# Second attention by pairs of heads: one float32 group per pair, exponentials ahead of the copies, ten projection steps before the first group

## The chip, the cores and the metric

The kernel runs on one core of a Trainium2 chip. The metric is the device time of one execution in microseconds (us). The core has a matrix engine (PE, with its weight loads PEld), a vector engine (DVE), an activation engine (ACT), a general engine (POOL, which also issues some DMAs) and a queue (SP) that issues most DMAs. Each works through its own instructions in order.

## What is computed

A two-layer decoder trunk on 256 positions of width 1024, all in float32. Each layer is a half-step SwiGLU feed-forward, a token mixer, and a second feed-forward, each with an RMS norm that is modulated by a conditioning vector. The mixer of the first layer is differential attention; the mixer of the second, which the change concerns, is forgetting attention with 16 heads of 64, keys `k`, values `v` and gates `F` shared and computed before:

```python
def forgetting_attention(h, w_q, w_o, k, v, F):
    q = (h @ w_q).reshape(b, s, B_HEADS, HEAD_DIM)
    ...
    def block(args):                       # 128 queries
        causal = q_pos[:, None] >= k_pos[None, :]
        decay = jnp.transpose(Fqb, (0, 2, 1))[..., None] - F_k[:, :, None, :]
        logits = jnp.einsum('bqhd,bkhd->bhqk', qb, k) * scale + decay
        logits = jnp.where(causal, logits, -jnp.inf)
        p = jax.nn.softmax(logits, axis=-1)
        return jnp.einsum('bhqk,bkhd->bqhd', p, v)
    ...
    return o.reshape(b, s, B_WIDTH) @ w_o
```

## The kernel before

Activations are held transposed: 128 features on the partitions, 256 positions along the free axis. A large product is made of three single-pass matmuls (`mm3`): weights and activations are each split into a high part (`wh`, `HH`, `obh`) and a rest (`wl`, `HL`, `obl`) in a rounded format, fp32r, and high x high, low x high and high x low are summed. The attention's own products (scores, transposes, values) run in full float32, each matmul as two instructions in the trace, transposes as one.

Weights stream in as pieces of 128x1024. For each, ACT casts `wh` from the raw piece and DVE subtracts to get `wl`. These background instructions are placed by a planner at emission (`bg`, `fill_act`, `fill_dve`): `InOrder` wraps PE, ACT, DVE and SP, keeps a running estimate of each engine's time, and puts a piece's cast or subtraction where it expects room. POOL isn't wrapped. What is emitted to an engine runs in that order.

The second attention (`attention_b`) stands between two feed-forwards. `late_pairs` projects q for the first eight heads (q0, q1) while the norm's factor is still being computed; meanwhile DVE and ACT make the modulated activations `HH` and `HL`, eight slices in turn (`MakeH`: `ht` and `HL` on DVE, `HH` on ACT), and at the end q1. Then 19 rounds `t` follow, one head per stage of a pipeline: the decay of head t+1 (DVE adds the key's gate `fkb`, which POOL's queue has loaded as 256 columns on all partitions, the query's gate `Fq` and the causal mask), the normalisation of head t-1 (DVE), the scores of head t (two matmuls over 64 rows, `sb`), DVE's reduction for the row maximum and ACT's exponentials, the transposes of head t-2 (`pwb`, copied by ACT to `wtb`), the values of head t-3 (`pob`, with v stationary and the weights moving). A pair's output is cast (`obh`) and subtracted (`obl`) in one piece each. `PLAN` says how many projection steps (`fills`) go before and after the scores in each round: 16 steps of six matmuls for q2 and q3 (heads 8 to 15), then 48 steps of three matmuls for the output projection (`OutProj.steps`, `pw`), which go through the first six pairs. `OutProj.finish` takes the last two pairs, with 48 matmuls. All instructions of PE, ACT, DVE and SP are recorded by a helper at L103, so the profile tells them apart by tiles.

The first attention (`attention_a`) is already written in groups: two 64-row halves' scores in turn (`s`), transposes (`pw<-tri,nl`), values with the transposed weights stationary (`po<-va,wt`), transposes of the output (`po<-tri,on`).

PSUM banks: `mmbank` has four, `sbank` (`sb`) two, `abank` and `bbank` one each.

Of the kernel before, what the change touches and what calls it, by code (L numbers as in the profile page):

```python
# [22 lines left out]
AH = 8  # L23
BH = 16
# [5 lines left out]
BIG = 3.0e38  # L30
# [9 lines left out]
CP_FIT = 0.9  # L40
DVE_FIT = 0.6
NFILL = 1
FRONT = 0
TAIL = 4
PLAN = [1, 1, 1, 1, 2, 1, 2, 3, 1, 3]
PACE = [0.62, 0.74, 0.62, 0.38, 0.76, 0, 0.74]
NRAW = 6
NLO = 5
# [59 lines left out]
def trunk(ctx, tc, a, out):  # L108
    nc = tc.nc
    InOrder.ready = {}  # L110
    pe = InOrder(tc, nc.tensor, 0.0, 1 / 2350)
    act = InOrder(tc, nc.scalar, 0.13, 1 / 1200)
    dve = InOrder(tc, nc.vector, 0.08, 1 / 960)
    sp = InOrder(tc, nc.sync, 0.0, 1 / 704)
    cp_ = ctx.enter_context(tc.tile_pool(name="cp", bufs=1))
# [15 lines left out]
    def bbank(name):  # L131
        return pp.tile([P, 512], F32, tag="tb", name=name)

    mm = pe.matmul
# [685 lines left out]
    QT = ((0, 128), (128, 256))  # L820
# [4 lines left out]
    ident, cmask, ub, skew, nlam, subg = (late[n] for n in ("ident", "cmask", "ub", "skew", "nlam", "subg"))  # L825
# [174 lines left out]
    op = attention_a()  # L1000
# [5 lines left out]
    kT = [cp_.tile([P, 512], F32, name=f"kT{j}") for j in range(4)]  # L1006
    vb = [[cp_.tile([P, 512], F32, name=f"vb{t}{nh}") for nh in range(2)] for t in range(2)]
# [17 lines left out]
    pz = sbank("pzf")[:, :S]  # L1025
# [13 lines left out]
    for i, (kk, n) in enumerate(v_proj("wkv", vb)):  # L1039
# [9 lines left out]
        if i == 3:  # L1049
# [4 lines left out]
            Fq = cp_.tile([P, 72], F32, name="Fq")[:, :2 * BH]  # L1054
# [6 lines left out]
            fdram = tc.dram_tile([BH, S], F32, name="fdram")  # L1061
# [12 lines left out]
    def attention_b():  # L1074
        ohs = [cp_.tile([P, 512], F32R, tag=f"hidh{j}", name=f"obh{j}") for j in range(4)]
        ols = [cp_.tile([P, 512], F32R, tag=f"hidl{4 + j}", name=f"obl{j}") for j in range(4)]
        o = [(ohs[c // 2][:, (c % 2) * 256:(c % 2) * 256 + 256],
              ols[c // 2][:, (c % 2) * 256:(c % 2) * 256 + 256]) for c in range(NC)]
        q = [cp_.tile([P, 512], F32, tag=f"hidl{j}", name=f"q{j}") for j in range(4)]
        gs, ds, sms = {}, {}, {}  # L1080

        def load_g(hd):
            g = cp_.tile([P, S], F32, tag=("hidh10", "hidl10", "hidl8", "hidl9")[hd % 4], name=f"fkb{hd}")
            nc.gpsimd.dma_start(g, bass.AP(fdram.tensor, fdram.offset + hd * S, [[0, P], [1, S]]))
            gs[hd] = g

        def decay(hd):
            d = cp_.tile([P, 384], F32, tag=f"hidh{4 + hd % 4}", name=f"d{hd}")
            for qt, (c0, w) in enumerate(QT):
                dve.scalar_tensor_tensor(  # L1090
                    d[:, c0:c0 + w], gs[hd][:, :w], Fq[:, qt * BH + hd:qt * BH + hd + 1], cmask[:, S - w:],
                    op0=ALU.add, op1=ALU.add)
            ds[hd] = d
            if hd + 4 < BH:
                load_g(hd + 4)

        late_pairs("wq", q[:2], ((1, 4), (1, 3)), AF.Exp)
        for hd in range(4):
            load_g(hd)
        decay(0)  # L1100
        op = OutProj(o)
        st = {}
        pob = {}
        mode[0] = "fill"

        def scores(hd):
            c, m = hd // 2, hd % 2
            rows = slice(m * HD, m * HD + HD)
            cb = (c % 2) * 256
            d = ds[hd]  # L1110
            s = sbank(f"sb{hd}")
# [3 lines left out]
            nm = kp.tile([P, 2], F32, tag="nm", name=f"nmb{hd}")  # L1115
            sm = kp.tile([P, 2], F32, tag="sm", name=f"smb{hd}")
            for qt, (c0, w) in enumerate(QT):
                dve.tensor_tensor_reduce(
                    d[:, c0:c0 + w], s[:, c0:c0 + w], d[:, c0:c0 + w], -0.125, BIG,
                    ALU.add, ALU.min, accum_out=nm[:, qt:qt + 1])  # L1120
                act.activation(d[:, c0:c0 + w], d[:, c0:c0 + w], AF.Exp,
                               bias=nm[:, qt:qt + 1], scale=-1.0, accum_out=sm[:, qt:qt + 1])
            sms[hd] = sm

        def normal(hd):
            d = ds[hd]
            rs = kp.tile([P, 2], F32, tag="rs", name=f"rsb{hd}")
            dve.reciprocal(rs, sms[hd])
            for qt, (c0, w) in enumerate(QT):
                dve.tensor_scalar(d[:, c0:c0 + w], d[:, c0:c0 + w], rs[:, qt:qt + 1], None, op0=ALU.mult)  # L1130

        def weights_t(hd):
            pw = abank(f"pwb{hd}")
            for b in range(3):
                pe.transpose(pw[:, b * P:b * P + P], ds[hd][:, b * P:b * P + P], ident)
            wt = cp_.tile([P, 384], F32, tag=f"hidh{8 + hd % 2}", name=f"wtb{hd}")
            act.copy(wt, pw[:, :384])
            st[hd] = wt

        def values(hd):  # L1140
            c, m = hd // 2, hd % 2
            rows = slice(m * HD, m * HD + HD)
            if m == 0:
                pob[c] = bbank(f"pob{c}")
            po, wt = pob[c], st[hd]
            vs = slice((hd % 8) * HD, (hd % 8) * HD + HD)
            v0, v1 = vb[0][hd // 8][:, vs], vb[1][hd // 8][:, vs]
            mm(po[rows, 128:256], v1, wt[:, 256:384], start=True, stop=False, skip_group_check=True)
            mm(po[rows, 0:256], v0, wt[:, 0:256], start=False, stop=True, skip_group_check=True)
            if m == 1:  # L1150
                oh, ol = o[c]
                act.copy(oh, po[:, :256])
                dve.tensor_tensor(ol, po[:, :256], oh.bitcast(F32), op=ALU.subtract)

        def fills():
            for j in (2, 3):
                yield from pair_proj("wq", q[j], f"pq{j}")
            for _ in range(6):
                yield from op.steps()

        fill = fills()

        def step(n):
            for _ in range(n):
                next(fill, None)

        step(FRONT)
        for t in range(BH + 3):
            n0, n1 = PLAN[2 * (t // 4):2 * (t // 4) + 2]
            step(n0)  # L1170
            if t + 1 < BH:
                decay(t + 1)
            if 0 <= t - 1 < BH:
                normal(t - 1)
            if t < BH:
                scores(t)
            step(n1)
            if 0 <= t - 2 < BH:
                weights_t(t - 2)
            if 0 <= t - 3 < BH:  # L1180
                values(t - 3)
        for i, n in fill:
            if i % 4 == 3:
                run_laters()
# [138 lines left out]
```

## Time and profile before

| | us |
|---|---|
| median of 3 runs | 1005.78 (1005.42 to 1006.49) |
| the profiled execution | 1006.43 |
| its span, first to last instruction | 1004.7 |
| first matmul behind late_pairs | 739.5 |
| last head's values end, projections alone from here | 805.6 |
| first matmul of the last feed-forward | 812.7 |

The granted clock is 0.997 over the span. Start times in the rows count from the span's first instruction. In a row of the timeline the duration of a matmul reaches from its start to its modelled end; matmuls are pipelined, so what one costs is read from the distance of starts. A row of the groups ends with busy us, mean ns of one, then the idle time before and who ended it.

### The profile page before, as it was taken

How to read it: one execution, taken by the hardware profiler on the slowest of the kernel's cores; microseconds unless marked ns; L12 is line 12 of the kernel's file. 1: busy time of each engine (PE TensorE's matmuls, PEld its weight loads, DVE VectorE, ACT ScalarE, POOL GpSimd, SP SyncE). 2: the span in 40 equal slices, each digit the busy share in tenths (PEclk: the TensorE clock that was granted, in tenths of full speed). 3: DMA queues.
4: the chain of work that ended last, by engine and by line, in shares of the span. 5: the costliest groups of instructions: out<-in, count | busy, mean ns of one | idle time of the engine just before them, and what ended most of it. 6: DMA issues, size and time to landing. Idle time of an engine off the chain costs nothing.

```text
span 1004.7 us, 20432 instructions
## 1 busy us (share of the span) xinstructions
PE 979.0 (97%) x8076; PEld 941.3 (94%) x8076; DVE 820.9 (82%) x1379; ACT 563.3 (56%) x922; POOL 37.1 (4%) x64
## 2 busy tenths in 40 slices
PE   5999999999999999999999999999999999999996
PEld 4999999988989999999988999999987799999996
DVE  6989979889889998888698988889897787555553
ACT  5465545575877645455476455454575576454552
POOL 0000100000111000000000000000011010000000
PEclk9999999999999999999999999999999999999998
DMA  8988999958765899888757999989744337665661
GB/s 347 414 333 285 334 364 345 348 199 320 264 211 196 272 403 356 288 283 308 275 191 304 363 339 327 331 296 336 245 147 122 107 125 236 198 193 153 172 183 43
DMA packets 68131, 265.08 MB, mean 264 GB/s; under 512 B 7961, under 2 KB 8113, under 8 KB 57922
## 3 DMA queue, kind: packets, MB, share of 16 engines
q1 hardware_dynamic: 65810, 258.31, 73.3%
q0 software_dynamic: 1792, 4.81, 1.8%
q8 instruction: 63, 1.03, 0.4%
q10 hardware_dynamic: 432, 0.64, 0.2%
q14 instruction: 34, 0.28, 0.1%
HBM read 262.66 MB, written 2.65 MB: 264 GB/s over the span
## 4 chain that ended last, share of the span: by engine, by line
PE 92%; DVE 3%; ACT 2%; issue 1%; DMA 1%; SPq 0%; POOL 0%; DVEq 0%; POOLq 0%; ACTq 0%
PE po L103 24%; PE pg L103 21%; PE pu L103 21%; PE pf L103 5%; PE pv L103 4%; PE pw L103 4%; PE lp L103 2%; PE pqk L103 2%; PE pk L103 1%; PE pob L103 1%; PE lg L103 1%; PE lu L103 1%; PE sb L103 1%; DVE wl L103 1%; DMA ada<-in_ada 1%
## 5 line engine op out<-in xcount | busy, mean ns | idle before, releaser
L103 DVE TENSOR_TENSOR wl<-raw,wh 128x1024 fp32r<-128x1024 f32 (+1 forms) x368 | 401.3, 1104 | 92.8 <-issue 24.7
L103 ACT CAST wh<-raw 128x1024 fp32r<-128x1024 f32 (+1 forms) x368 | 349.3, 958 | 208.7 <-PE pu L103 96.5
L103 DVE CUSTOM_DVE_ANT_0 ada<-ada,cact,vecs 128x1024 f32<-128x1024 f32 x160 | 203.3, 1278 | 0.0
L103 PE MATMUL po<-hidl,wh 128*128 128x256 f32 x704 | 194.3, 276 | 0.0
L103 PE MATMUL po<-hidh,wh 128*128 128x256 f32 x704 | 194.3, 276 | 0.0
L103 PE MATMUL po<-hidh,wl 128*128 128x256 f32 x704 | 194.3, 276 | 0.0
L103 PE MATMUL pg<-HH,wh 128*128 128x256 f32 x608 | 168.1, 276 | 0.0
L103 PE MATMUL pg<-HH,wl 128*128 128x256 f32 x608 | 168.0, 276 | 0.0
L103 PE MATMUL pg<-HL,wh 128*128 128x256 f32 x608 | 168.0, 276 | 0.0
L103 PE MATMUL pu<-HH,wl 128*128 128x256 f32 x608 | 167.9, 276 | 0.0
L103 PE MATMUL pu<-HH,wh 128*128 128x256 f32 x608 | 167.9, 276 | 0.0
L103 PE MATMUL pu<-HL,wh 128*128 128x256 f32 x608 | 167.9, 276 | 0.0
L103 PEld LDWEIGHTS po<-hidh,wh 128*128 128x128 f32 x704 | 132.2, 188 | 0.0
L103 PEld LDWEIGHTS po<-hidh,wl 128*128 128x128 f32 x704 | 132.2, 188 | 0.0
L103 PEld LDWEIGHTS po<-hidl,wh 128*128 128x128 f32 x704 | 132.2, 188 | 0.0
L103 PEld LDWEIGHTS pg<-HH,wh 128*128 128x128 f32 x608 | 114.2, 188 | 0.7 <-issue 0.6
L103 PEld LDWEIGHTS pg<-HH,wl 128*128 128x128 f32 x608 | 114.2, 188 | 0.0
L103 PEld LDWEIGHTS pu<-HL,wh 128*128 128x128 f32 x608 | 114.2, 188 | 0.0
L103 PEld LDWEIGHTS pu<-HH,wl 128*128 128x128 f32 x608 | 114.1, 188 | 0.0
L103 PEld LDWEIGHTS pg<-HL,wh 128*128 128x128 f32 x608 | 114.1, 188 | 0.0
L103 PEld LDWEIGHTS pu<-HH,wh 128*128 128x128 f32 x608 | 114.1, 188 | 0.0
L103 ACT ACTIVATE HH<-ht,modall 128x256 fp32r<-128x256 f32 x56 | 27.8, 507 | 40.4 <-DVE ht L103 38.9
(204 smaller groups left out, 1604.7 us busy)
## 6 DMA issues: line engine op xcount, KB each, us to landing
raw<-in_win SPq DMA_DIRECT2D x176, 512.0 KB, 5.9
ada<-in_ada SPq DMA_DIRECT2D x79, 1024.0 KB, 7.4
raw<-in_wout SPq DMA_DIRECT2D x64, 384.0 KB, 4.9
raw<-in_wout SPq DMA_DIRECT2D x64, 320.0 KB, 4.3
raw<-in_wqk SPq DMA_DIRECT2D x16, 512.0 KB, 5.0
raw<-in_wo SPq DMA_DIRECT2D x16, 512.0 KB, 5.2
raw<-in_wv SPq DMA_DIRECT2D x8, 512.0 KB, 7.4
raw<-in_wkk SPq DMA_DIRECT2D x8, 512.0 KB, 8.1
```

The source lines that it names most:

```text
L103: return self.tc.keep_in_program_order(f(*args, **kw))
```

## The change

The second attention is rewritten like the first one, with a pair of heads in place of a head:

- `scores` writes the causal mask of the diagonal blocks into both banks with two fp32r matmuls (identity x mask), then adds four float32 score matmuls, the two heads' row halves in turn. Two ACT copies (`identr`, `maskr`) behind `late_pairs` make the operands.
- `decay` moves to POOL, as one `tensor_scalar` per block (key's gate plus query's gate, no mask), and loads 512 columns per pair.
- The weights are no longer normalised on DVE; `divide` scales a pair's output by the reciprocal sums.
- `values` makes the transposed weights stationary and moves 64 columns of v, so the output comes with positions on the partitions, and two more transposes (`out_t`) turn it; `out_split` casts and subtracts in two halves.
- One group per pair holds scores, transposes, values and output transposes of four successive pairs without a projection step between. On ACT and DVE `exps` comes first, then `out_split`, then the copies.
- Eleven groups with 10, 8, 8, 6, 7, 7, 7, 7, 7, 6 and 5 steps before them; a step of q2 and q3 counts as two.

```diff
-FRONT = 0
-TAIL = 4
-PLAN = [1, 1, 1, 1, 2, 1, 2, 3, 1, 3]
...
+        identr = cp_.tile([P, P], F32R, tag="hidl8", name="identr")
+        maskr = cp_.tile([P, P], F32R, tag="hidl9", name="maskr")
+        def load_g(c):
+            g = cp_.tile([P, 512], F32, tag=("hidh10", "hidl10")[c % 2], name=f"fkb{c}")
+            nc.gpsimd.dma_start(g, bass.AP(fdram.tensor, fdram.offset + 2 * c * S, [[0, P], [1, 2 * S]]))
...
-        def decay(hd):
-            d = cp_.tile([P, 384], F32, tag=f"hidh{4 + hd % 4}", name=f"d{hd}")
-            for qt, (c0, w) in enumerate(QT):
-                dve.scalar_tensor_tensor(
-                    d[:, c0:c0 + w], gs[hd][:, :w], Fq[:, qt * BH + hd:qt * BH + hd + 1], cmask[:, S - w:],
-                    op0=ALU.add, op1=ALU.add)
+        def decay(c):
+            for m in range(2):
+                hd = 2 * c + m
+                d = cp_.tile([P, 384], F32, tag=f"hidh{4 + hd % 4}", name=f"d{hd}")
+                for qt, (c0, w) in enumerate(QT):
+                    nc.gpsimd.tensor_scalar(d[:, c0:c0 + w], gs[c][:, m * S:m * S + w],
+                                            Fq[:, qt * BH + hd:qt * BH + hd + 1], None, op0=ALU.add)
...
         late_pairs("wq", q[:2], ((1, 4), (1, 3)), AF.Exp)
+        act.copy(identr, ident)
+        act.copy(maskr, cmask[:, P:])
...
+        def scores(c, sb):
+            cb = (c % 2) * 256
+            m2 = maskr.rearrange("p (o k) -> p o k", o=1).to_broadcast([P, 2, P])
+            for m in range(2):
+                diag = sb[m].rearrange("p (a b) -> p a b", b=256)[:, :, :P]
+                mm(diag, identr, m2, start=True, stop=False, skip_group_check=True)
             for qt, (c0, w) in enumerate(QT):
-                mm(s[:, c0:c0 + w], q[c // 2][rows, cb + qt * P:cb + qt * P + P],
-                   kT[c // 2][rows, cb:cb + w], start=True, stop=True)
+                for m in range(2):
+                    rows = slice(m * HD, m * HD + HD)
+                    mm(sb[m][:, c0:c0 + w], q[c // 2][rows, cb + qt * P:cb + qt * P + P],
+                       kT[c // 2][rows, cb:cb + w], start=False, stop=qt == 1, skip_group_check=True)
...
-        def normal(hd):
-            dve.reciprocal(rs, sms[hd])
-            for qt, (c0, w) in enumerate(QT):
-                dve.tensor_scalar(d[:, c0:c0 + w], d[:, c0:c0 + w], rs[:, qt:qt + 1], None, op0=ALU.mult)
...
+        def values(c, po):
+            for m in range(2):
+                ...
+                mm(po[:, m * HD:m * HD + HD], wt[0], v0, start=True, stop=True)
+                mm(po[:, P + m * HD:P + m * HD + HD], wt[1], v0, start=True, stop=False)
+                mm(po[:, P + m * HD:P + m * HD + HD], wt[2], v1, start=False, stop=True)
...
+        def group(t):
+            ...
+            if cs is not None:
+                scores(cs, sb)
+            if cw is not None:
+                weights_t(cw, ta, tb)
+            if cv is not None:
+                values(cv, tb[:, 256:])
+            if co is not None:
+                pz = [sb[m][:, 384:] for m in range(2)]
+                out_t(co, pz)
+            if cs is not None:
+                exps(cs, sb)
+            if co is not None:
+                out_split(co, pz)
+            if cw is not None:
+                weights_out(cw, ta, tb)
+            if cv is not None:
+                divide(cv, tb[:, 256:])
+            if t + 1 < NP:
+                decay(t + 1)
...
+        for t, n in enumerate((10, 8, 8, 6, 7, 7, 7, 7, 7, 6, 5)):
+            for _ in range(n):
+                next(fill)
+            group(t)
```

PE before, one round in the middle of the attention (`sb` scores, `pq` a projection step, `pwb` transposes, `pob` values):

```order
L103 MATMUL sb_9600<-kT_6350,q_9247 128x128
L103 MATMUL sb_9600<-kT_6350,q_9247 128x256
L103 MATMUL pq_9580<-HH,wh 128x256
L103 MATMUL pq_9580<-HH,wl 128x256
L103 MATMUL pq_9580<-HL,wh 128x256
...
L103 MATMUL pwb_9617<-tri,d_9476 128x128 x3
L103 MATMUL pob_9577<-wtb_9575,vb_6355 64x128
L103 MATMUL pob_9577<-wtb_9575,vb_6353 64x256
```

PE after the change, group 4 (masks, scores, `wa` and `wb` transposes and values, `onb` the output's first transpose):

```order
L100 MATMUL sb_0_9771<-maskr,identr 128x2x128
L100 MATMUL sb_1_9772<-maskr,identr 128x2x128
L100 MATMUL sb_0_9771<-kT_6351,q_9248 128x128
L100 MATMUL sb_1_9772<-kT_6351,q_9248 128x128
L100 MATMUL sb_0_9771<-kT_6351,q_9248 128x256
L100 MATMUL sb_1_9772<-kT_6351,q_9248 128x256
L100 MATMUL wa_9773<-tri,d_9659 128x128 x3
L100 MATMUL wa_9773<-tri,d_9662 128x128
L100 MATMUL wb_9774<-tri,d_9662 128x128 x2
L100 MATMUL wb_9774<-vb_6353,wta_9724 128x64 x2
L100 MATMUL wb_9774<-vb_6355,wta_9724 128x64
...
L100 MATMUL sb_0_9771<-tri,onb_9730 128x128
```

The two heads' scores alternate between two banks behind two masks, and no projection stands inside (the other value matmuls are left out, and a second `onb` transpose follows).

ACT at the end of late_pairs, before (`lcol` and `q` finish q1):

```order
L103 COPY lcol<-lp_9323 128x1
L103 ACTIVATE q_9247<-lt,lcol 128x256 x2
L103 CAST wh<-raw 128x1024
L103 ACTIVATE d_9436,smb_9457<-d_9436,nmb_9456 128x128
L103 ACTIVATE d_9436,smb_9457<-d_9436,nmb_9456 128x256
```

and after:

```order
L100 COPY lcol<-lp_9325 128x1
L100 ACTIVATE q_9247<-lt,lcol 128x256 x2
L100 CAST identr<-tri 128x128
L100 CAST maskr<-tri 128x128
L100 CAST wh<-raw 128x1024
L100 ACTIVATE d_9436,smb_9488<-d_9436,nmb_9487 128x128
```

The copies of the identity and of the mask stand behind q1 and ahead of the first exponentials.

POOL at the start of the attention, before nothing but loads (`fkb`), and after:

```order
L1084 DMA fkb_9432<-fdram 128x512
L1084 DMA fkb_9434<-fdram 128x512
L1093 TENSOR_SCALAR d_9436<-fkb_9432,Fq 128x128
L1093 TENSOR_SCALAR d_9436<-fkb_9432,Fq 128x256
L1093 TENSOR_SCALAR d_9439<-fkb_9432,Fq 128x128
L1093 TENSOR_SCALAR d_9439<-fkb_9432,Fq 128x256
L1084 DMA fkb_9442<-fdram 128x512
L1093 TENSOR_SCALAR d_9499<-fkb_9434,Fq 128x128
```

The first two pairs' decays need only the loads; that of the third waits for the first pair's transposes, since it reuses their tiles.

More of the change, by code (lines that the diff above doesn't have):

```diff
@@ L1080, in attention_b @@
         gs, ds, sms = {}, {}, {}
[L1082 to L1085, printed above, removed]
-        def decay(hd):
-            d = cp_.tile([P, 384], F32, tag=f"hidh{4 + hd % 4}", name=f"d{hd}")
-            for qt, (c0, w) in enumerate(QT):
-                dve.scalar_tensor_tensor(
-                    d[:, c0:c0 + w], gs[hd][:, :w], Fq[:, qt * BH + hd:qt * BH + hd + 1], cmask[:, S - w:],
-                    op0=ALU.add, op1=ALU.add)
-            ds[hd] = d
-            if hd + 4 < BH:
-                load_g(hd + 4)
+        identr = cp_.tile([P, P], F32R, tag="hidl8", name="identr")
[3 more added lines that the diff above has]
+            nc.gpsimd.dma_start(g, bass.AP(fdram.tensor, fdram.offset + 2 * c * S, [[0, P], [1, 2 * S]]))
+            gs[c] = g
+        def decay(c):
[5 more added lines that the diff above has]
+                                            Fq[:, qt * BH + hd:qt * BH + hd + 1], None, op0=ALU.add)
+                ds[hd] = d
+            if c + 2 < BH // 2:
+                load_g(c + 2)
         late_pairs("wq", q[:2], ((1, 4), (1, 3)), AF.Exp)
-        for hd in range(4):
-            load_g(hd)
+        act.copy(identr, ident)
+        act.copy(maskr, cmask[:, P:])
+        for c in range(2):
+            load_g(c)
         decay(0)
@@ L1102, in attention_b @@
         st = {}
-        pob = {}
         mode[0] = "fill"
-        def scores(hd):
-            c, m = hd // 2, hd % 2
-            rows = slice(m * HD, m * HD + HD)
+        NP = BH // 2
+        def scores(c, sb):
             cb = (c % 2) * 256
-            d = ds[hd]
-            s = sbank(f"sb{hd}")
+            m2 = maskr.rearrange("p (o k) -> p o k", o=1).to_broadcast([P, 2, P])
+            for m in range(2):
+                diag = sb[m].rearrange("p (a b) -> p a b", b=256)[:, :, :P]
+                mm(diag, identr, m2, start=True, stop=False, skip_group_check=True)
@@ L1140, in values @@
[L1140 to L1153, printed above, removed]
+                for m in range(2):
+                    rows = slice(m * HD, m * HD + HD)
+                    mm(sb[m][:, c0:c0 + w], q[c // 2][rows, cb + qt * P:cb + qt * P + P],
+                       kT[c // 2][rows, cb:cb + w], start=False, stop=qt == 1, skip_group_check=True)
@@ new lines, in exps @@
+        def exps(c, sb):
+            nm = kp.tile([P, 4], F32, tag="nm", name=f"nmb{c}")
+            sm = kp.tile([P, 4], F32, tag="smb", name=f"smb{c}", bufs=3)
+            for m in range(2):
+                d = ds[2 * c + m]
+                for qt, (c0, w) in enumerate(QT):
+                    cc = 2 * qt + m
+                    dve.tensor_tensor_reduce(
+                        d[:, c0:c0 + w], sb[m][:, c0:c0 + w], d[:, c0:c0 + w], -0.125, BIG,
+                        ALU.add, ALU.min, accum_out=nm[:, cc:cc + 1])
+                    act.activation(d[:, c0:c0 + w], d[:, c0:c0 + w], AF.Exp,
+                                   bias=nm[:, cc:cc + 1], scale=-1.0, accum_out=sm[:, cc:cc + 1])
+            sms[c] = sm
@@ new lines, in weights_t, with weights_out @@
+        def weights_t(c, ta, tb):
+            for j in range(6):
+                d, b = ds[2 * c + j // 3], j % 3
+                pe.transpose(ta[:, j * P:j * P + P] if j < 4 else tb[:, (j - 4) * P:(j - 3) * P],
+                             d[:, b * P:b * P + P], ident)
+        def weights_out(c, ta, tb):
+            w0 = cp_.tile([P, 512], F32, tag="hidh8", name=f"wta{c}")
+            w1 = cp_.tile([P, 256], F32, tag="hidh9", name=f"wtb{c}")
+            act.copy(w0, ta)
+            dve.tensor_copy(w1, tb[:, :256])
+            st[c] = [w0[:, j * P:j * P + P] for j in range(4)] + [w1[:, j * P:j * P + P] for j in range(2)]
@@ new lines, in values @@
+        def values(c, po):
+            for m in range(2):
+                hd = 2 * c + m
+                wt = st[c][3 * m:3 * m + 3]
+                vs = slice((hd % 8) * HD, (hd % 8) * HD + HD)
+                v0, v1 = vb[0][hd // 8][:, vs], vb[1][hd // 8][:, vs]
+                mm(po[:, m * HD:m * HD + HD], wt[0], v0, start=True, stop=True)
+                mm(po[:, P + m * HD:P + m * HD + HD], wt[1], v0, start=True, stop=False)
+                mm(po[:, P + m * HD:P + m * HD + HD], wt[2], v1, start=False, stop=True)
@@ new lines, in divide, with out_t @@
+        def divide(c, po):
+            rs = kp.tile([P, 4], F32, tag="rs", name=f"rsb{c}")
+            dve.reciprocal(rs, sms[c])
+            on = kp.tile([P, 256], F32, tag="w512b", name=f"onb{c}")
+            dve.tensor_tensor(on.rearrange("p (g d) -> p g d", g=4), po.rearrange("p (g d) -> p g d", g=4),
+                              rs.rearrange("p (g o) -> p g o", o=1).to_broadcast([P, 4, HD]), op=ALU.mult)
+            st[c] = on
+        def out_t(c, pz):
+            for qt in range(2):
+                pe.transpose(pz[qt], st[c][:, qt * P:qt * P + P], ident)
@@ new lines, in out_split @@
+        def out_split(c, pz):
+            oh, ol = o[c]
+            for qt in range(2):
+                act.copy(oh[:, qt * P:qt * P + P], pz[qt])
+            for qt in range(2):
+                qs = slice(qt * P, qt * P + P)
+                dve.tensor_tensor(ol[:, qs], pz[qt], oh[:, qs].bitcast(F32), op=ALU.subtract)
+        def group(t):
+            cs, cw, cv, co = (c if 0 <= c < NP else None for c in (t, t - 1, t - 2, t - 3))
+            sb = [sbank(f"sb{t}_{m}") for m in range(2)] if cs is not None or co is not None else None
+            ta = abank(f"wa{t}") if cw is not None else None
+            tb = bbank(f"wb{t}") if cw is not None or cv is not None else None
+            if cs is not None:
[17 more added lines that the diff above has]
+                decay(t + 1)
@@ L1155, in fills @@
         def fills():
             for j in (2, 3):
-                yield from pair_proj("wq", q[j], f"pq{j}")
+                for _ in pair_proj("wq", q[j], f"pq{j}"):
+                    yield
+                    yield
             for _ in range(6):
-                yield from op.steps()
+                for _ in op.steps():
+                    yield
         fill = fills()
-        def step(n):
+        for t, n in enumerate((10, 8, 8, 6, 7, 7, 7, 7, 7, 6, 5)):
             for _ in range(n):
-                next(fill, None)
@@ L1167, in attention_b @@
[L1167 to L1184, printed above, removed]
+                next(fill)
@@ L1185, in attention_b @@
+            group(t)
+        for _ in fill:
+            pass
         return op
```

18 lines of the change are left out of this document (removed).

## The prediction

> **What bounds the kernel now.** I read first the busy time by stretch. Its row for most of the second attention (start and end in us, its length, then busy us and instructions of PE, PEld, DVE, ACT and POOL, clock, DMA share, GB/s):
>
> ```profile
> 768.00:806.00 38.00, 38.00 (x241) 28.28 (x240) 25.71 (x83) 20.16 (x56) 1.69 (x3) 1.00 0.36 109
> ```
>
> PE is busy all 38 us at full clock, DVE 68%, ACT 53%, POOL 4%, DMA 36%. Then the waits of PE between 735 and 813 us (who waited, for whom; total, times, longest):
>
> ```profile
> PE sb L103 <- DVE nmb L103: 1.0, 1, 1.0
> PE pwb L103 <- ACT wtb L103: 0.5, 1, 0.5
> ```
>
> Only 1.5 us can come back from waits; anything more must come out of PE's own work. Third, the chain of waits through one head (start, us, what):
>
> ```profile
> 757.30 0.85 PE sb L103 x4
> 758.14 0.90 PE pq L103 x6
> 759.04 0.33 PE pwb L103 x3
> 759.37 0.80 PE pob L103 x4
> 760.16 0.90 PE pq L103 x6
> 761.06 0.85 PE sb L103 x4
> ```
>
> The chain never leaves PE: scores, a projection step, transposes, values, a step. A head costs 761.06 - 757.30 = 3.76 us with 12 projection matmuls in it. Last, PE's timeline at the first matmul behind late_pairs, in the closing run of projections, and where the feed-forward takes over:
>
> ```profile
> 739.48 0.28 PE L103 MATMUL pq<-HH,wh 128*128 128x256 f32 x1
> ...
> 806.01 0.28 PE L103 MATMUL pw<-obh,wh 128*128 128x256 f32 x1
> ...
> 812.72 0.28 PE L103 MATMUL lg<-HH,wh 128*128 128x258 f32 x1
> ```
>
> From 806.01 to 812.72 are 57 projection matmuls: 0.118 us each. The stage is 812.72 - 739.48 = 73.2 us. In it are 96 matmuls for q2 and q3, 144 in the six output steps and 48 in finish, 288 x 0.118 = 33.9 us, which stay. The heads' own PE time is 73.2 - 33.9 - 1.5 = **37.8 us**, 2.36 a head. The single head agrees: 3.76 - 12 x 0.118 = 2.34.
>
> **PE after the change.** The first attention already works as the new code does: scores of two 64-row halves in turn, and values with the transposed weights stationary. One of its groups on PE's timeline:
>
> ```profile
> 251.72 0.28 PE L103 MATMUL pqk<-HL,wh 128*128 128x256 f32 x1
> 251.93 0.93 PE L103 MATMUL s<-qk 64*128 64x128 f32 x8
> 252.79 0.55 PE L103 MATMUL pw<-tri,nl 128*128 128x128 f32 x3
> 253.17 0.83 PE L103 MATMUL po<-va,wt 128*128 128x128 f32 x6
> 253.84 0.38 PE L103 MATMUL po<-tri,on 128*128 128x128 f32 x2
> ...
> 254.18 0.28 PE L103 MATMUL pqk<-HH,wl 128*128 128x256 f32 x1
> ```
>
> Eight score instructions take 252.79 - 251.93 = 0.86 us, as long as the four of one head above (0.85): the two halves run side by side. The whole group takes 254.18 - 251.72 less two projection matmuls, 2.22 us, with 3 transposes, 6 value instructions and 2 transposes of the output. The new pair adds to this: two mask matmuls, 0.24 if they cost what a 256-column projection matmul costs; three more transposes, 0.33 by the pwb row; six more value instructions. Those stream 64 columns, a width that the trace lacks; the rows on both sides are 128 columns (0.67 us for six, 253.17 to 253.84) and 16:
>
> ```profile
> 529.21 0.73 PE L103 MATMUL pF<-lft,tri 128*128 128x16 f32 x6
> 529.88 0.39 PE L103 MATMUL pFk<-tri,lft 128*16 128x128 f32 x2
> ```
>
> Six take 0.67 us there too, so 64 columns cost the same 0.112 each. Sum: 2.22 + 0.24 + 0.33 + 0.67 = 3.46 us a pair against 4.7, eight pairs 27.7, and 0.2 for group 0, whose scores go straight back to projections: 27.9. **PE's work falls by 37.8 - 27.9 = 9.9 us.** For the masks, a form that the trace lacks, the cheap end is 0.12 and the dear end the float32 price of the sb row (0.85 us for 384 columns), 0.57: up to 0.9 more a pair. I take the cheap end, since operands and width are those of a projection matmul.
>
> **The waits.** The two old ones go: the bank that freed late (sb) and the copy that the transposes waited for (pwb) were both DVE and ACT starting heads behind a queue, and group 1 now comes eight steps after group 0. What is late next is the start. PE reaches group 0 after ten steps, 30 matmuls: 739.48 + 3.54 = 743.0. Its first instruction reads maskr, which ACT copies behind q1. The rows for q1, and the nearest to a 128x128 copy on ACT (from the groups, mean ns):
>
> ```profile
> 744.01 0.91 ACT L103 ACTIVATE q<-lt,lcol 128x256 f32<-128x256 f32 x2 [0.84 <-DVE lt L103]
> L103 ACT ACTIVATE on<-po 128x128 f32<-128x128 f32 x16 | 4.1, 260 | 2.1 <-PE po L103 2.1
> ```
>
> 744.92 + 2 x 0.26 = 745.4, so PE waits **2.4 us**, with everything behind it: its queue is in order, and q's steps 5 to 7, which could run, stand behind the masks.
>
> And q1 may itself come later. The decays move from DVE to POOL, and the first two pairs' eight tensor_scalars run during late_pairs, as soon as the first loads land (DMA issues: median us to landing) and POOL has started them:
>
> ```profile
> 726.12 1.22 POOL L1084 DMA_DIRECT2D fkb<-fdram  x2 [194.21 <-PE po L103]
> fkb<-fdram POOLq DMA_DIRECT2D x4, 128.0 KB, 5.6
> L442 POOL TENSOR_TENSOR acc<-acc,sq 128x256 f32<-128x256 f32 x10 | 7.9, 790 | 1.7 <-ACT sq L103 1.1
> L1017 POOL MEMSET fgh<- 128x512 f32 x2 | 1.1, 529 | 171.5 <-PE po L103 171.5
> ```
>
> Not before 731.7. A 256-column tensor_scalar lies between the memset's 0.26 and the two-input add's 0.79; four of a pair (768 columns) between 0.8 and 2.4 us. DVE is then on the chain that makes HH, HL and q1, without a gap (period 0.92, two instructions of 0.48):
>
> ```profile
> 737.39 0.48 DVE L103 SCALAR_TENSOR_TENSOR ht<-x,modall,r 128x256 f32<-128x256 f32 x1
> 738.31 0.49 DVE L103 SCALAR_TENSOR_TENSOR ht<-x,modall,r 128x256 f32<-128x256 f32 x1
> ...
> 810.94 0.57 DVE L103 SCALAR_TENSOR_TENSOR HL<-x,modall,HH 128x256 fp32r<-128x256 f32 x1
> 813.09 0.56 DVE L103 SCALAR_TENSOR_TENSOR HL<-x,modall,HH 128x256 fp32r<-128x256 f32 x1
> ```
>
> The last two stand beside POOL's adds, and are 0.08 longer. The adds:
>
> ```profile
> 810.42 0.80 POOL L442 TENSOR_TENSOR acc<-sq,sq 128x256 f32<-128x256 f32 x1 [34.94 <-ACT sq L103]
> 812.57 0.80 POOL L442 TENSOR_TENSOR acc<-acc,sq 128x256 f32<-128x256 f32 x1
> ```
>
> HL ended at 811.51 and 813.65, 0.28 to 0.29 after the adds' ends at 811.22 and 813.37: it looks held until POOL is done, then runs. So a POOL instruction beside this chain costs up to its length. The chain's scaling starts at 735.7; I reckon that decay(0) is through by then and decay(1) partly not: between 0 and 2.4 us, I take **1.0**. [...]
>
> Third, group 3 is followed at once by output step 0, which needs the pair that group 3 has only just transposed. Before, at the last pair, PE's values and what followed on ACT and DVE:
>
> ```profile
> 804.76 0.86 PE L103 MATMUL pob<-wtb,vb 128*64 128x128 f32 x4
> 805.66 0.37 ACT L103 CAST obh<-pob 128x256 fp32r<-128x256 f32 x1 [1.68 <-PE pob L103]
> 806.07 0.42 DVE L103 TENSOR_TENSOR obl<-pob,obh 128x256 fp32r<-128x256 f32 x1 [2.38 <-ACT obh L103]
> ```
>
> obl ended 0.87 us after the values. With casts and subtractions in halves about the same: 0.8 us of wait after group 3, which no step separates, 0.5 after group 4 (one step of 0.35 us), 0.1 after group 5, none later: **1.4**. That the exponentials stand ahead of these casts on ACT costs nothing, as four of them end about when out_t does.
>
> POOL later: decay(t+1) may start when group t's transposes are done, about 1.9 us into it, and is read 1.2 us into group t+1; the period is 3.46 + 7 x 0.353 = 5.9, which leaves 5.2 us for 0.8 to 2.4. DVE loses decay and normalisation work, and the weight splits ride on it with room. The stages behind are PE's alone and only start earlier.
>
> **Sum:** -9.9 - 1.5 + 2.4 + 1.0 + 1.4 = -6.6 us. The profiled execution took 1006.43 (span 1004.7), which gives 999.8; from the median of the runs, 1005.78, it is 999.2. I give 999.5.
>
> **Rivals.** (1) *Fewer new waits.* POOL is through before the chain starts, and the casts come in half the time: 1.0 + 0.7 less, 997.8. For it: 4 us lie between landing and 735.7. Against: the held HL rows. (2) *A long idle makes PE slow.* At the program's start PE came from an idle of 3.8 us and ran at half rate:
>
> ```profile
> 17.12 0.41 PE L103 MATMUL pf<-HH,wh 128*128 128x256 f32 x1
> 17.33 0.41 PE L103 MATMUL pf<-HH,wl 128*128 128x256 f32 x1
> ...
> 22.24 0.32 PE L103 MATMUL pf<-HH,wh 128*128 128x256 f32 x1
> ```
>
> 0.21 a matmul from 17.12 to 22.24, 24 of them, each 0.095 dearer: 2.3 us. [...] Against: the two waits in this stage were too short to show it. [...] (3) *The PE saving isn't had*: the score halves don't overlap when they add onto a mask (8 x 0.86 = 6.9), or the masks cost float32's price (8 x 0.9 = 7.2): about 1006.6. Against: the first attention's rows; for it, no matmul there adds onto a bank already written. (4) *POOL sets the period*, and the kernel is slower. It decides from the point where a pair's decays and load issue (0.6) outlast 5.9 us by the 1.4 a group that eats 8.3 us over groups 2 to 7: 6.7 us for four instructions, 2.8 times the add's price. At 7.5 us it would be 6 x 2.2 = 13 us more, 1012.5. Only an unknown cost of this instruction speaks for it.
>
> **Chances.** Forecast 0.58 (its own range 998.5 to 1002), (1) 0.17, (2) 0.09, (3) 0.10, (4) 0.06. The range holds the first three: low 996.5, a further microsecond below (1) for PE terms a little smaller, high 1003.5, the dear ends of ports and casts together. 0.2%, about what a measurement tells from no change, is 2.0 us: faster (below 1003.8) 0.84, same 0.10, slower 0.06.
>
> **What would show it.** PE: eight sb instructions in 0.86 us behind masks 0.12 apart; 12 value instructions in 1.34; a pair's group in 3.5. One wait of 2 to 4 us on ACT's maskr near 743, two or three under 1 us on obh or obl near 763 to 776, no sb or wa wait after. POOL: tensor_scalars between 0.26 and 0.79 for 256 columns, two pairs of them between 731 and 738; ht and HL there longer than 0.48. I am wrong if PE waits in every group, if POOL's work per pair passes 5 us, or if the stage ends with less than 3 or more than 9.5 us gained.

## The result, and the profile after

| | before | after |
|---|---|---|
| median, first runs (4 each) | 1005.6 us (1004.2 to 1006.5) | 1019.2 us (1015.7 to 1028.0) |
| median, later runs | 1008.2 us (18 runs, 1003.5 to 1012.6) | 1016.3 us (5 runs, 1014.9 to 1022.8) |
| profiled execution; its span | 1006.43; 1004.7 us | 1015.69; 1013.9 us |
| first matmul behind late_pairs | 739.48 us | 739.58 us |
| last feed-forward starts | 812.72 us | 821.88 us |
| the stage between these two | 73.24 us | 82.30 us |

The change makes the kernel slower: ratio 1.0122, 95% interval 1.008 to 1.0163. The forecast was 999.5 and faster. In the profiled executions 9.1 of the 9.3 us of loss lie in the stage: it was to fall from 73.2 to 66.6 us and took 82.30, while what follows it takes 191.9 and 192.0 us in the two traces. The stretch that was quoted of before has this row in the changed kernel (start and end, length, busy us and instructions of PE, PEld, DVE, ACT, POOL, clock, DMA share, GB/s):

```profile
768.00:806.00 38.00, 30.89 (x216) 27.99 (x216) 14.64 (x56) 14.66 (x50) 9.89 (x14) 0.87 0.23 70
```

PE was busy all 38 us at clock 1.00 before. Now it idles for 7 us of them and its clock is 0.87. So two things are lost, time in which PE waits and time in which it runs slowly. Its waits from 735 to 830 us (who waited, for whom; total, times, longest):

```profile
PE pw L100 <- ACT obh L100: 9.4, 5, 2.6
PE sb L100 <- ACT maskr L100: 3.5, 1, 3.5
```

The second was forecast (2.4, and 1.0 for POOL's decays beside ht and HL). The first was forecast as 1.4 in three waits. The chain of waits shows what it consists of, at group 3 (start, us, what):

```profile
765.94 0.24 PE sb L100 x2
766.18 0.02 issue
766.20 0.23 DVE d L100
766.42 0.09 DVE nmb L100
766.51 0.02 issue
766.53 1.86 ACT d L100 x8
768.40 0.32 ACT obh L100 x2
768.71 0.04 issue
768.76 4.29 PE pw L100 x21
```

PE ends out_t; only then does DVE begin the reductions of the *other* pair, whose scores were ready long before; then ACT's four exponentials (eight instructions, 1.86 us); only then the two casts that PE waits for. DVE's timeline shows why the reductions are so late: group 2, which has no out_t, and group 3, which has one (in brackets, idle time before and who ended it):

```profile
758.74 0.28 DVE L100 CUSTOM_DVE_ANT_0 d<-sb,d 128x128 f32<-128x128 f32 x1
...
766.20 0.29 DVE L100 CUSTOM_DVE_ANT_0 d<-sb,d 128x128 f32<-128x128 f32 x1 [4.57 <-PE sb L100]
```

`out_t` writes columns 384 and on of the very `sb` banks whose first 384 columns the reductions read. `group` emits out_t first, and the reductions wait for the last write to the tile, not for the columns that they read: they start at 766.20, behind out_t's matmuls from 765.77 on, though the transposes follow the scores from 763.77 on. The trace shows it in the semaphores too, the signals by which one engine releases another: group 2's last two score matmuls raise one, group 3's score matmuls raise none, and its out_t does. PE's timeline around that wait:

```profile
762.59 0.40 PE L100 MATMUL sb<-maskr,identr 128*128 128x256 f32 x2
762.91 0.93 PE L100 MATMUL sb<-kT,q 64*128 64x128 f32 x8
763.77 0.66 PE L100 MATMUL wa<-tri,d 128*128 128x128 f32 x4
764.27 0.38 PE L100 MATMUL wb<-tri,d 128*128 128x128 f32 x2
764.49 1.00 PE L100 MATMUL wb<-vb,wta 128*128 128x64 f32 x8
765.33 0.61 PE L100 MATMUL wb<-vb,wtb 128*128 128x64 f32 x4
765.77 0.39 PE L100 MATMUL sb<-tri,onb 128*128 128x128 f32 x2
768.76 0.45 PE L100 MATMUL pw<-obh,wh 128*128 128x256 f32 x1 [2.59 <-ACT obh L100]
...
769.93 0.41 PE L100 MATMUL pw<-obl,wh 128*128 128x256 f32 x1
770.14 0.41 PE L100 MATMUL pw<-obh,wh 128*128 128x256 f32 x1
...
772.55 0.28 PE L100 MATMUL pw<-obh,wh 128*128 128x256 f32 x1
772.66 0.28 PE L100 MATMUL pw<-obh,wl 128*128 128x256 f32 x1
```

The group itself costs what was forecast: scores 0.86 (762.91 to 763.77), values 1.28 (764.49 to 765.77). Behind the wait the matmuls start 0.21 us apart, and from 772.4 on 0.11 apart again. There are four such spells of half rate in the stage: behind the wait for maskr and behind the obh waits of groups 3, 4 and 5. The granted clock, third from the end in these rows, dates the first two:

```profile
746.81:748.46 1.65, 1.65 (x13) 1.18 (x14) 0.17 (x2) 0.89 (x1) 0.00 (x0) 1.00 0.25 67
748.46:751.87 3.41, 3.41 (x19) 3.41 (x18) 2.58 (x10) 2.80 (x9) 0.00 (x0) 0.50 0.42 138
768.94:772.35 3.41, 3.41 (x17) 3.41 (x18) 2.10 (x5) 1.19 (x2) 0.00 (x0) 0.50 0.33 99
```

Each lasts 3.41 us, and the first begins only 1.65 us after the wait for maskr has ended at 746.81. The granted clock over the whole span is on record for every run, and so tells of spells where no trace was kept: it is 0.997 for the traces without a spell, 0.996 with one, 0.994 with two, and 0.99 with the four here.

### The profile page after: what moved, and what is told of

Its sections match the earlier page's. It is cut to its first block, busy times and chain, and to the rows that moved or that the text cites. A ratio compares the mean times of both kernels' runs of the same rounds, so it can differ in the third digit from the quotient of the medians.

```text
span 1013.9 us, 20539 instructions
## 1 busy us (share of the span) xinstructions
PE 975.7 (96%) x8140; PEld 948.9 (94%) x8140; DVE 808.8 (80%) x1331; ACT 560.5 (55%) x924; POOL 58.2 (6%) x88
## 4 chain that ended last, share of the span: by engine, by line
PE 89%; ACT 3%; DVE 3%; DMA 2%; issue 1%; POOL 0%; SPq 0%; DVEq 0%; POOLq 0%; ACTq 0%
PE po L100 23%; PE pg L100 20%; PE pu L100 20%; PE pf L100 5%; PE pv L100 4%; PE lp L100 3%; PE pw L100 3%; PE pk L100 1%; PE pqk L100 1%; PE wb L100 1%; PE lu L100 1%; PE lg L100 1%; PE sb L100 1%; DVE wl L100 1%; DMA ada<-in_ada 1%
```

## The experiments

Stage is, as above, the time from the first matmul behind late_pairs to the first of the last feed-forward in the profiled run. The first four kernels ran on one chip, beside before at a median of 1007.7 us (31 runs); the last four on another, beside 1008.2.

| kernel | median, us | ratio to before | stage, us |
|---|---|---|---|
| copies first | 1004.2 | 0.9957 (0.9935 to 0.998) | 69.27 |
| exponentials ahead of out_t | 1005.2 | 0.9977 (0.9952 to 1.0002) | 65.65 |
| mask copies early | 1012.3 | 1.005 (1.0018 to 1.0081) | 75.88 |
| wait filled | 1018.4 | 1.0096 (1.0064 to 1.0128) | 80.94 |
| exponentials and mask copies moved | 998.9 | 0.9885 (0.9855 to 0.9914) | 62.88 |
| first decays on DVE | 1001.6, one run | none | 64.83 |
| wait half filled | 1014.1 | 1.0071 (1.0039 to 1.0102) | 75.77 |
| the changed kernel again | 1016.3 | 1.0091 (1.0056 to 1.0126) | 82.72 |

### The copies first

```diff
-            if cs is not None:
-                exps(cs, sb)
             if co is not None:
                 out_split(co, pz)
...
             if cv is not None:
                 divide(cv, tb[:, 256:])
+            if cs is not None:
+                exps(cs, sb)
```

> Edit: in a group the exponentials are emitted last, behind out_split, the weight copies and divide, instead of ahead of them. Profiled run of the changed kernel: 1015.69, PE waits 9.4 us for obh in five waits and 3.5 us for maskr, and runs at half rate for about 3.5 us behind four of these waits (about 1.75 us lost each, 7 in all). Theory A (the reductions wait for out_t because out_t writes the same sb tile, the exponentials follow, and the casts of obh stand behind them; a wait of over 2.5 us then halves PE's rate): the obh waits fall to 1 to 2.5 us in all, none over 1 us, the three spells behind them go, maskr's wait and its spell stay: 1015.7 - 8 - 5.3 = about 1002.5 (1001 to 1004.5). Rival B (the half rate has nothing to do with the waits): the waits go, the spells stay: about 1007.7. Rival C (the loss is POOL's decays or the start): 1012 or more.

PE's waits in its trace:

```profile
PE sb L100 <- ACT maskr L100: 3.0, 1, 3.0
PE pw L100 <- ACT obh L100: 0.4, 1, 0.4
```

The obh waits are all but gone, and with them the half-rate spells behind them; the one behind maskr is still there. Further waits in the stage, for ACT's `d` and DVE's `nmb`, are of 0.2 us each, 0.8 in all. The median is 1004.2 us, as theory A had it, and B and C fall. The obh wait is even shorter than the forecast's own 1.4.

### The exponentials ahead of out_t

```diff
+            if cs is not None:
+                exps(cs, sb)
             if co is not None:
                 pz = [sb[m][:, 384:] for m in range(2)]
                 out_t(co, pz)
-            if cs is not None:
-                exps(cs, sb)
```

> Edit: the exponentials stay ahead of the copies, but are emitted ahead of out_t, so they need not wait for it; out_t must then wait for DVE's four reductions. Theory A: the reductions start right behind the scores, 2 us of transposes and values cover them, the exponentials end about when out_t does, and the obh waits fall to 1 to 3 us in all: 1001.5 to 1005. Rival D (casts behind exponentials are too late whatever the reductions wait for): obh waits stay above 1 us each, 5 us or more in all, time 1009 or more. Rival E (out_t now waits for the reductions): a new PE wait of 0.5 us or more in each of five groups.

DVE's and ACT's timelines at group 3, whose scores start at 760.02 and whose out_t starts at 762.87 in this trace, and PE's waits:

```profile
761.08 0.29 DVE L100 CUSTOM_DVE_ANT_0 d<-sb,d 128x128 f32<-128x128 f32 x1 [2.35 <-PE sb L100]
...
763.19 0.43 ACT L100 CAST obh<-sb 128x128 fp32r<-128x128 f32 x2
```

```profile
PE sb L100 <- ACT maskr L100: 3.1, 1, 3.1
PE pw L100 <- ACT obh L100: 0.4, 1, 0.4
```

The reductions start right behind the scores, the exponentials are through as out_t ends, and the casts follow. Exponentials ahead of the copies are therefore harmless in themselves; harmful is that they stand ahead of the casts *and* behind out_t. Rivals D and E fall: no wait of PE for the reductions appears. The stage is 65.65, 1 us under the forecast 66.6. The median, 1005.2, is just above what was expected, and the runs go from 999.9 to 1010.7. In the profiled one the last feed-forward took 198.3 us (804.42 to 1002.7) instead of 192.0; more on that below.

### The mask copies early

```diff
+        act.copy(identr, ident)
+        act.copy(maskr, cmask[:, P:])
         late_pairs("wq", q[:2], ((1, 4), (1, 3)), AF.Exp)
-        act.copy(identr, ident)
-        act.copy(maskr, cmask[:, P:])
```

> Edit: the two copies for identr and maskr are emitted ahead of late_pairs; nothing else. Theory A: the 3.5 us wait near 743 goes, and with it the half-rate spell behind it (1.75): 1015.7 - 5.2 = about 1010.4; waits for obh stay as they are. If the spell isn't due to the wait: about 1012.2. If the copies now hold up ACT in late_pairs, or q1 is what group 0 really waits for: 1014 or more.

The wait for maskr is gone and nothing takes its place; the obh waits are 9.4 as before. The stage is 6.4 us shorter than the changed kernel's, 1.2 more than expected: a spell of half rate is missing behind group 3 too. PE's timeline there:

```profile
763.16 0.38 PE L100 MATMUL pw<-obh,wh 128*128 128x256 f32 x1 [2.59 <-ACT obh L100]
...
763.99 0.28 PE L100 MATMUL pw<-obl,wh 128*128 128x256 f32 x1
764.10 0.28 PE L100 MATMUL pw<-obh,wh 128*128 128x256 f32 x1
```

The same wait of 2.59 us that halved the rate in the changed kernel doesn't halve it here. The median, 1012.3, is 2 us above the expected 1010.4.

### The wait filled, and half filled

```diff
             group(t)
+            if 3 <= t <= 7:
...
+                for _ in range(24):
+                    tc.keep_in_program_order(nc.tensor.matmul(
+                        op.out(0), zer, hn[0][0], start=t == 3, stop=False, skip_group_check=True))
```

The zero weights are the unmasked half of `cmask`, copied with the mask; the second kernel has 10 in place of 24.

> Edit: behind each of groups 3 to 7 PE gets 24 further fp32r matmuls of 256 columns with zero weights (24 x 0.118 = 2.8 us), added onto an accumulator of the output projection, so that PE works through the time in which it waited for obh; the result is unchanged. Theory A with the clock: PE has no idle time over 1 us behind these groups, the half-rate spells behind them go although the added work takes as long as the waits did: 1015.7 - 3 x 1.75 + at most 3 (for groups whose wait was shorter than the added work) = 1010 to 1014, and projection matmuls at 0.118 right behind the added ones. Rival B (half rate not due to idleness, but to what these matmuls are or to what ACT and DVE do then): projection matmuls at 0.21 there as before, 1016 to 1021.

> Edit: as the filled wait, with 10 zero-weight matmuls (1.18 us) behind each of groups 3 to 7 in place of 24, so that they stand inside the wait and lengthen nothing. Theory A with the clock: PE's gaps shrink from 2.87, 2.52, 2.16, 1.82 and 1.46 us to 1.7 or less, none of them is followed by matmuls at 0.21, and the stage takes 82.3 - 3 x 1.75 = about 77 us, although obh lands no sooner. Rival B (gaps of any length over 1 us do it, or the gap isn't the cause): spells behind at least two of them, 80 to 82 us.

PE's timeline with 24 (L1226 is the added line), and then with 10:

```profile
762.87 3.12 PE L1226 MATMUL pw<-HH,maskr 128*128 128x256 f32 x24
765.83 0.28 PE L100 MATMUL pw<-obh,wh 128*128 128x256 f32 x1
...
767.00 0.28 PE L100 MATMUL pw<-obh,wh 128*128 128x256 f32 x1
767.11 0.28 PE L100 MATMUL pw<-obh,wl 128*128 128x256 f32 x1
```

```profile
765.61 1.43 PE L1226 MATMUL pw<-HH,maskr 128*128 128x256 f32 x10
768.45 0.39 PE L100 MATMUL pw<-obh,wh 128*128 128x256 f32 x1 [1.41 <-ACT obh L100]
...
769.38 0.28 PE L100 MATMUL pw<-obh,wh 128*128 128x256 f32 x1
769.50 0.28 PE L100 MATMUL pw<-obh,wl 128*128 128x256 f32 x1
```

In both traces the projections behind the groups run at full rate, 0.11 to 0.12 us apart behind the first few. The half-filled kernel is the clean one: from out_t to the first projection there pass 2.99 us, as in the changed kernel (765.77 to 768.76; here 765.46 to 768.45), so obh lands no sooner, and only PE's idleness is broken up. Its stage is 75.77, 6.5 us shorter. Of this 0.4 is a shorter wait for maskr (3.1 against 3.5). The other 6.1 are four spells of 1.5 us: the three behind the groups, and that behind maskr, which is missing in this run though its wait was left as it was. Its clock between 768 and 806 us is 1.00:

```profile
768.00:806.00 38.00, 35.44 (x293) 32.44 (x294) 17.56 (x65) 17.01 (x56) 9.95 (x14) 1.00 0.25 75
```

So matmuls that do nothing save 6.1 us of the profiled stage. The median is 2.3 us lower (1014.1 against 1016.3), but the two intervals overlap, so a saving of time isn't shown by the medians. The clocks do show fewer spells over all runs: 0.994 to 0.997 with the wait half filled, 0.994 to 0.996 with it filled, 0.989 to 0.991 in all nine runs of the changed kernel. The profiled run, at 0.997, is the only one of the half-filled kernel's ten at that clock. The filled kernel's stage is 80.94, 1.4 us shorter, which about fits: 24 x 0.118 x 5 = 14.2 of added work in place of 10.8 of gaps, less three spells of 1.5. Its median, 1018.4, missed the expected 1010 to 1014 and lies in rival B's range; against B stands the trace, where no row of matmuls behind the groups is 0.21 apart. In its profiled run the last feed-forward took 198.3 us.

### Both moved

The edits of the second and third kernel together.

> Edit: exponentials ahead of out_t and the two mask copies ahead of late_pairs, together. From the first matmul behind late_pairs to the first of the last feed-forward, the stage took 73.24 us before, 82.30 changed, 65.65 with the exponentials moved (3.1 of it the wait for maskr). Theory A: the two edits add, 62.5 us and no PE wait over 0.5 us, which is 10.7 us under before; the run's time about 995 where the last feed-forward goes at 113 ns a matmul as in before's trace, 1001.5 where it goes at 118. Rival F (behind the wait for maskr stands another, for HL or for the first decays): the wait shrinks to 1 to 2 us, the stage 64 us or more.

PE's waits are 0.6 us in all, and PE is busy 62.20 of the stage's 62.87 us:

```profile
PE pw L100 <- ACT obh L100: 0.4, 1, 0.4
PE sb L100 <- DVE nmb L100: 0.2, 1, 0.2
```

```profile
742.48:805.35 62.87, 62.20 (x530) 57.63 (x529) 43.19 (x138) 41.20 (x120) 27.18 (x35) 1.00 0.41 126
```

The stage is 62.88 us, 10.4 under before, where 62.5 was expected; rival F falls. At 998.9 us (994.8 to 999.1) it is the fastest of all kernels, ahead of before by 0.9 to 1.5%. All six runs have a clock of 0.997 or 0.998, like before: where the long waits are gone, so is the half rate. The profiled run took 999.1, not the expected 995, although its last feed-forward goes at 113 ns: the stage starts at 742.48, 3.0 us later than in before. A first feed-forward that goes at 118 for half its length would give that, by estimate.

### The first decays on DVE

```diff
-                    nc.gpsimd.tensor_scalar(d[:, c0:c0 + w], gs[c][:, m * S:m * S + w],
+                    (dve if c < 2 else nc.gpsimd).tensor_scalar(d[:, c0:c0 + w], gs[c][:, m * S:m * S + w],
```

This stands on top of the exponentials ahead of out_t.

> Edit: exponentials ahead of out_t, and the decays of the first two pairs (eight tensor_scalars) on DVE behind late_pairs instead of on POOL during it. If POOL's decays held up the ht and HL instructions (ht 0.54, HL 0.57 us mean in the changed kernel, 0.48 in before): both 0.48 to 0.50 in late_pairs, q1 about 1.4 us earlier against the first matmul behind late_pairs, and the wait for maskr 1.6 to 2.4 us instead of 3.1. If not: 3.1 as before. The eight instructions cost DVE 1.5 to 3 us ahead of the first reductions, which nothing waits for.

The groups of DVE in the changed kernel, and in this one (730 to 746 us; they end with busy us, mean ns, then idle time before), and this kernel's wait:

```profile
L100 DVE SCALAR_TENSOR_TENSOR HL<-ht,modall,HH 128x256 fp32r<-128x256 f32 x8 | 4.6, 571 | 0.5 <-ACT HH L100 0.2 <-ACT lcol L100 0.2
L100 DVE SCALAR_TENSOR_TENSOR ht<-x,modall,r 128x256 f32<-128x256 f32 x8 | 4.3, 541 | 0.2
```

```profile
L100 DVE SCALAR_TENSOR_TENSOR ht<-x,modall,r 128x256 f32<-128x256 f32 x8 | 3.8, 483 | 0.2
L100 DVE SCALAR_TENSOR_TENSOR HL<-ht,modall,HH 128x256 fp32r<-128x256 f32 x7 | 3.4, 480 | 0.3 <-ACT HH L100 0.3
```

```profile
PE sb L100 <- ACT maskr L100: 2.3, 1, 2.3
```

Without POOL's decays beside them ht and HL take 0.48 again, and the wait for maskr is 2.3 us, against 3.1 with the decays on POOL and 3.5 in the changed kernel. The contention on DVE is shown. Against the kernel that this one stands on the wait is 0.8 us shorter, within what was expected, and q1 starts 0.8 us earlier against the first matmul behind late_pairs, not 1.4. As a single run it says nothing on the time.

### The changed kernel again

> The changed kernel as it is, on the chip of the three above, since its runs so far lie between 1015.7 and 1028. Theory A: the profile again shows half-rate spells behind some but not all of the waits of 2.2 to 3.5 us, not the same ones; the stage 77 to 83 us; and where two runs differ by 6 us or more, it is the pace of the last feed-forward (113 or 118 ns a matmul) besides. Median 1014 to 1022.

The waits are the same (9.5 and 3.2), the stage is 82.72, with half-rate spells behind the same four waits, where other ones had been expected. Its clock of 0.989 is that of five lengths of 3.41 us rather than four (0.990; an estimate from before's 0.997 and the 0.50 of a spell), so one of the four may have lasted twice as long. This profiled run took 1022.37 us, 6.7 more than the first one, and its first matmul behind late_pairs starts at 745.88 instead of 739.58: 6.3 of the 6.7 were lost before the stage, in the first feed-forward.

## Why the prediction was wrong

**The step that failed** is the sentence "That the exponentials stand ahead of these casts on ACT costs nothing, as four of them end about when out_t does." They end 2.2 us after out_t (768.39 against 766.18 at group 3), since DVE's reductions, which feed them, don't start behind the scores but behind out_t. The prediction took the time of the reductions from the scores' end and didn't ask which writes to `sb` are emitted ahead of them. The obh term, put at 1.4, came to 9.4: 8.0 of the 15.7 us by which the stage (82.30) missed its forecast (66.6). It recurs five times and not three, because a wait of 2.6 us shrinks by only 0.35 a group (one more projection step stands ahead of the next pair each time); it ends with group 7, the last that has exponentials. With the exponentials ahead of out_t, or behind the casts, it is 0.4, less than forecast.

**A rival was under-priced.** Rival (2), that idleness makes PE slow, was given 9% and one spell of 2.3 us, 999.5 + 2.3 = 1001.8. The mechanism acted four times, 1.5 us each, 6.1 in all: 13.65 us of the stage ran at half rate, with matmuls 0.213 apart in place of 0.118. The half-filled wait shows that it is the idleness. It was held back because the trace of before shows it behind an idle of 3.76 us at the program's start alone, and the two waits of its stage, 1.0 and 0.5 us, were too short to show it. These are the gaps between the start of the last instruction ahead of a wait and of the first behind it, over the changed kernel's two traces and those of the experiments:

| gap, us | followed by half rate | not |
|---|---|---|
| 3.26 to 3.88 | 4 | 2 |
| 2.16 to 2.87 | 8 | 2 |
| 1.34 to 1.83 | 0 | 8 |

The traces give the length of a spell, 3.41 us for each of the four in the changed kernel's first trace. They don't show how long a wait must be: eight gaps of under 2.9 us were enough, while one of 3.38 us passed without a spell (742.06 to 745.44 with the exponentials ahead of out_t), and so did the one at maskr, a wait of 3.1 us, in the half-filled kernel. Nor does a spell begin at a fixed distance from its wait: the first begins 1.65 us after its wait has ended, the second 0.18 us (768.94 against 768.76). What decides between the two stays open.

**The sum after the fact.** 62.2 of PE's work (65.65 less waits of 0.4 and 3.1, where no spell fell), 9.4 and 3.5 of waits, 6.1 of half rate make 81.2 of the 82.30 measured. The remaining 1.1 isn't accounted for.

**What was right.** PE's work: 61.8 forecast (33.9 and 27.9), 62.2 measured; masks 0.12 apart, scores 0.86, values 1.28 (forecast 1.34). So rival (3) fell, and the saving is real: 9.9 us were forecast, and 9.5 are had (73.24 less 1.5 of waits, against 62.2). The wait for maskr: 3.4 forecast, 1.0 of it for POOL's decays beside ht and HL, 3.5 measured. That share is 0.8 to 1.2 by the first decays on DVE. The forecast's range calls it ports; no run shows ports. What the runs show is ht and HL at 0.48 without POOL's work beside them and 0.54 to 0.57 with it, so that the two engines hinder each other here. That HL is held until POOL is done and then runs, as the prediction read its rows, isn't shown: HL ended 0.28 us after the adds and takes 0.48 alone, and the longest of ht and HL beside POOL's decays took 0.87. That nothing is waited for on sb or wa later held too.

**POOL's price was outside the bounds given**, though nothing hung on it. A 256-column tensor_scalar was put between 0.26 and 0.79 us:

```profile
L1093 POOL TENSOR_SCALAR d<-fkb,Fq 128x256 f32<-128x256 f32 x4 | 3.8, 942 | 0.0
L1093 POOL TENSOR_SCALAR d<-fkb,Fq 128x128 f32<-128x128 f32 x4 | 3.2, 812 | 4.2 <-DMA fkb<-fdram 4.1
```

These are those of the first two pairs, beside DVE; from the fifth pair on they take 0.91 to 0.92 and 0.59 to 0.60. With 3.0 to 3.9 us a pair POOL stays below the period of 5.9, so that rival (4) fell.

## What to carry to other kernels

Ask of every instruction that reads part of a shared bank which writes to the whole of it are emitted ahead: a late write to other columns can hold up a reader whose data has long been there (here DVE's reductions at group 3, which start at 766.20 though the scores end at 763.8), and everything behind that reader in the engine's queue. When PE's work shrinks, it meets waits that it didn't reach before; price each not by its length alone but also with the half rate that may follow: here it followed 12 of 16 gaps of 2.16 us or more and none of eight of 1.83 or less, and cost 1.5 us a spell in the changed kernel. Where such a wait can't be removed, breaking it up can be worth even matmuls that do nothing: 6.1 us of the profiled stage here, though not shown by the medians.

## What the runs showed of the hardware

Besides full and half rate PE shows two paces 4% apart in these traces, 0.113 and 0.118 us between starts, and a run may keep either through a whole feed-forward. Rows of the groups between 860 and 960 us of two kernels with the same code there, the one with both edits and the one with the exponentials moved (count, busy us, mean ns):

```profile
L100 PE MATMUL pu<-HH,wl 128*128 128x256 f32 x100 | 27.6, 276 | 0.0
```

```profile
L100 PE MATMUL pu<-HH,wl 128*128 128x256 f32 x100 | 28.1, 281 | 0.0
```

The starts are 0.113 us apart in the first and 0.118 in the second, without any wait, and from the last feed-forward's first matmul to the end of the span, with 1592 matmuls between, 192.0 or 198.3 us pass. The pace may also change within one: with both edits the stage starts 3.0 us later than in before, about half of the 6 us between the two paces (an estimate). The changed kernel's two profiled runs differ by it in the first feed-forward, and such steps of 6 us are about as large as the scatter of a kernel's runs in the experiments (1003.5 to 1012.6 for before). What chooses the pace stays open. It may be why the medians of the first two experiments don't follow their stages (69.27 and 65.65), and it is why the stages are compared first here. A second reason is on record: the second kernel's profiled run is the only one of its ten at a clock of 0.997, the others are at 0.994 to 0.996, so that by the clock a spell or two fell in each of them. Behind which waits isn't on record, but the stage of 65.65 is then a good case and not the usual one.
